# Longer weight part buffers, and a 32-byte offset for the parts of some stationary weight blocks

## The chip, the cores and the metric

The kernel runs on one core of a Trainium2 chip. The metric is the device time of one execution in microseconds (us), as the median of several runs; one more execution was recorded by the hardware profiler.

## The reference, cut to what matters

Two decoder layers on 256 tokens of width 2048. Layer 0 is a Mamba-2 mixer, layer 1 a sparse attention mixer; each ends in a residual and a layer norm. Nearly all the work is matrix products in float32 with large weights that are used once:

```
proj = x @ w_in                 # 2048 x 10304 (layer 0)
...                             # conv, scan by chunks, gate, group norm
h0 = yg @ w_out                 # 4096 x 2048
x1 = layer_norm(alpha * x + h0)
proj = x1 @ w_in                # 2048 x (512 + 336 + 4096): q and kv latents, gates
q, q_lat, o = small products per head with w_uq, w_uk, w_uv (32 heads)
out = layer_norm(alpha * x1 + (o * silu(gate)) @ w_out)   # 4096 x 2048
```

## The kernel before, in words

**Units.** All large weights come as a stream of 404 blocks ("units") of 128 partitions by 1024 float32 values (672 for the kv latent). The class `Stream` loads each into a `raw` buffer (pool `wraw`, four buffers), and `convert` makes two parts of it in a format that TensorE multiplies at a higher rate than float32: `hi`, a rounded copy made by ScalarE (L98), and `lo`, the rest, made by VectorE (L106). `hi` and `lo` lie in pools `whi` and `wlo` of four buffers each, so unit i uses the fifth, sixth ... buffer again in turn (i modulo 4). Some units around the two layer ends get their parts from pools of their own (`st.homes`: pools `wmore`, six buffers, and `wlast`, four): the last two blocks of the first output product, the first four of the q latent, the first two of the kv latent, and the last four of the second output product.

**How a unit is used on TensorE.** A matmul has a stationary operand (128 columns, loaded ahead by a weight load) and a moving operand that streams past it. There are two kinds of unit:

- *Stationary units* (`stream_w`: the input projection of layer 0, tile `acc`, and the gates of layer 1, tile `g`; also `idx_pe`, `pair_b` and the first half of `pair_a`): slices of 128 columns of `hi` and `lo` are the weights, the activations move. In `stream_w` a unit has eight matmuls of `hi` against 512 moving columns (L285) and eight of `lo` against 256 (L282). Two units make one output: the first runs `hi` and then `lo`, the second `lo` and then `hi`. The next pair so begins with `hi` where the last one ended with `hi`.
- *Moving units* (`out_proj`, L512 to L514, and `stream_tok`, L640 to L642): the activations are the weights, and 512 columns of `hi` or `lo` move (336 for the kv latent; 256 in the tail). The change calls these units "wide".

In `pair_a` the first 512 columns of the unit are stationary (key, L822 to L824) and the others move in slices of 256 (value, L831 to L833).

**What sets the order.** The order is written out: the program runs unit after unit, and smaller steps (convolution, norms, heads) are stepped in between. TensorE executes its list in that order.

**Where the operands lie.** Byte addresses within a partition, as the built program has them, taken modulo 64:

| operand | start modulo 64 before | after |
|---|---|---|
| `hi`, `lo` in `whi`, `wlo` (four buffers each) | 0 | 0, or 32 for the units that the change moves |
| `hi`, `lo` in `wmore`, `wlast` | 32 | 0 |
| activations of `stream_w` and of `out_proj` (`xT`, `x1T`, `yg`, `og`) | 0 | 0 |
| latents (`cqT`, `ckvT`), head operands (`hk`, `hq`, `hv`, `prT`) | 32 | 32 |

The slices that a matmul takes of them begin whole multiples of 64 bytes further on. Before, all buffers of `raw`, `hi` and `lo` and the activations `xT` start at the same place modulo 4096 as well; after, the four buffers of a pool start 64 bytes further on from one to the next, modulo 4096.

Of the kernel before, what the change touches and what calls it, by code (L numbers as in the profile page):

```python
# [10 lines left out]
F32R = mybir.dt.float32r  # L11
# [5 lines left out]
P = 128  # L17
# [34 lines left out]
EARLY = 8  # L52
# [5 lines left out]
class Unit:  # L58


    def __init__(self, src, width, pe):
        self.src, self.width, self.pe = src, width, pe


class Stream:
# [7 lines left out]
        self.limit = 1 << 30  # L73
        self.homes = {}

    def add(self, src, width, pe):
        self.units.append(Unit(src, width, pe))
        return len(self.units) - 1

    def side(self, i, gen):  # L80
        self.starts.setdefault(i, []).append(gen)
# [8 lines left out]
    def convert(self, i, eng, later=False):  # L90

        if i < len(self.units):
            w = self.units[i].width
            r = self.raws.pop(i)
            ph, pl = (self.homes[i],) * 2 if i in self.homes else (self.whi, self.wlo)
            h = ph.tile([P, 1024], F32R, tag="hi", name=f"hi{i}")
            l = pl.tile([P, 1024], F32R, tag="lo", name=f"lo{i}")
            self.nc.scalar.activation(h[:, :w], r[:, :w], AF.Copy)  # L98
            self.parts[i] = (h, l)
            self.halfway[i] = (l[:, :w], r[:, :w], h[:, :w].bitcast(F32))  # L100
        if not later:
            self.finish(i, eng)
# [34 lines left out]
def trunk_kernel(ctx: ExitStack, tc: tile.TileContext, x, xt, w1, wdt, dtp, prm, wo1,  # L137
# [14 lines left out]
    st = Stream(nc, wraw, whi, wlo)  # L152
    v = nc.vector

    def acc_tile(name):
        return p_acc.tile([P, 512], F32, tag="acc", name=name)
# [112 lines left out]
    def stream_w(half, cell, name):  # L269


        def pe(h, l):
            if half == 0:
                cell["ps"] = acc_tile(name)
            ps, xs = cell["ps"], cell["x"][0]
            first, second = (0, 1) if half == 0 else (1, 0)
            for lo in (first, second):
                for k in range(8):
                    kt, w = half * 8 + k, slice(k * P, (k + 1) * P)
                    last = half == 1 and lo == second and k == 7  # L280
                    if lo:
                        nc.tensor.matmul(ps[:, 0:T], l[:, w], xs[:, kt, 0:T], start=False,  # L282
                                         stop=last, skip_group_check=True)
                    else:
                        nc.tensor.matmul(ps, h[:, w], xs[:, kt, :], start=(kt == 0), stop=last,  # L285
                                         skip_group_check=True)
        return pe
# [194 lines left out]
    for g in range(NG):  # L482
        for kind, n in (("B", 1), ("C", 1), ("x", 4), ("z", 4)):
            for ci in range(n):
                cell = {"x": xcell}
                for half in range(2):
                    k = len(st.units)
                    i = st.add(w1[k], 1024, stream_w(half, cell, f"acc{k}"))
# [7 lines left out]
    def out_proj(arr, act, name, evac, lead, tail, hold):  # L496

        cells = [{} for _ in range(4)]  # L500

        def mm(n, kb, h, l, half, part=None, cols=(0, 512), first=0):

            c0, c1 = cols
            ps = cells[n]["ps"][half][:, c0:c1] if part is None else part
            for k in range(2):
                kk = kb * 2 + k
                a = act[kk // 16][:, kk % 16, :]
                ah = a[:, half * P:(half + 1) * P]
                al = a[:, T + half * P:T + (half + 1) * P]  # L510
                hs, ls = h[:, k * 512 + c0:k * 512 + c1], l[:, k * 512 + c0:k * 512 + c1]
                nc.tensor.matmul(ps, ah, hs, start=(kk == 2 * first), stop=False)  # L512
                nc.tensor.matmul(ps, ah, ls, start=False, stop=False)  # L513
                nc.tensor.matmul(ps, al, hs, start=False, stop=(kk == 31))  # L514

        held = []

        def unit(n, kb):
            def pe(h, l):
                if kb == 0:  # L520
                    mk = (acc_tile, y_tile)[n % 2]
                    cells[n]["ps"] = [mk(f"{name}{n}_{j}") for j in range(2)]
                mm(n, kb, h, l, 0)
                if n == 3 and kb >= 16 - hold:
                    held.append((n, kb, h, l))
                    if kb == 15:
                        tail(cells[n], held, mm)
                else:
                    mm(n, kb, h, l, 1)
            i = st.add(arr[n * 16 + kb], 1024, pe)  # L530
            if kb == 15 and n < 3:
                for half in range(2):
                    st.side(i, (evac, n, half, cells[n]))

        for n in (0, 1):
            for kb in range(lead):
                unit(n, kb)
        for n in (0, 1):
            for kb in range(lead, 16):
                unit(n, kb)  # L540
        for n in (2, 3):
            for kb in range(16):
                unit(n, kb)
# [87 lines left out]
    def stream_tok(kb, width, cell, name, held=None):  # L631

        def mm(kb, h, l, half):
            ps = cell["ps"][half][:, 0:width]
            for k in range(2):
                kt = kb * 2 + k
                ah = X1[0][:, kt, half * P:(half + 1) * P]
                al = X1[0][:, kt, T + half * P:T + (half + 1) * P]
                hs, ls = h[:, k * width:(k + 1) * width], l[:, k * width:(k + 1) * width]
                nc.tensor.matmul(ps, ah, hs, start=(kt == 0), stop=False)  # L640
                nc.tensor.matmul(ps, ah, ls, start=False, stop=False)
                nc.tensor.matmul(ps, al, hs, start=False, stop=(kt == 15))  # L642

        def pe(h, l):
            if kb == 0:
                cell["ps"] = [acc_tile(f"{name}{j}") for j in range(2)]
            mm(kb, h, l, 0)
            if held is None:
                mm(kb, h, l, 1)
                return  # L650
            held.append((kb, h, l))
            L["early"](kb)
            if len(held) == EARLY:
                for a in held:
                    mm(*a, 1)
                st.limit = 1 << 30
                st.convert_to(n_o1 + EARLY + 4)
        return pe
# [78 lines left out]
    cells = {"kv": {}, "q": {}}  # L737
    held = []
    for kb in range(8):
        i = st.add(wcq[kb], 1024, stream_tok(kb, 512, cells["q"], "qp",  # L740
                                             held if kb < EARLY else None))
    st.side(i, (lat_norm, cells["q"], 512, PC_QG, 4, "q", "cqT"))
    for kb in range(8):
        i = st.add(wkv[kb], 672, stream_tok(kb, 336, cells["kv"], "kvp"))
    st.side(i, (lat_norm, cells["kv"], 256, PC_KVG, 2, "kv", "ckvT"))
    st.side(i, (kidx_steps, cells["kv"]))
    gates = iter(range(NH2))
# [4 lines left out]
    def idx_pe(q, cell):  # L752
        def pe(h, l):
            cell["ps"] = acc_tile(f"ix{q}")
            for k in range(2):
                ps = cell["ps"][:, k * T:(k + 1) * T]
                for kt in range(4):
                    o = (k * 4 + kt) * P
                    nc.tensor.matmul(ps, h[:, o:o + P], cqT[:, kt, 0:T], start=(kt == 0), stop=False)
                    nc.tensor.matmul(ps, h[:, o:o + P], cqT[:, kt, T:2 * T], start=False, stop=False)  # L760
                    nc.tensor.matmul(ps, l[:, o:o + P], cqT[:, kt, 0:T], start=False, stop=(kt == 3))
        return pe
# [41 lines left out]
    for q in range(4):  # L804
        cell = {}
        i = st.add(wix[q], 1024, idx_pe(q, cell))
# [30 lines left out]
    def pair_b(p):  # L837
        def pe(h, l):
            pq = s_tile(f"q{p}")
            for k in range(2):  # L840
                ps = pq[:, k * T:(k + 1) * T]
                for kt in range(4):
                    o = (k * 4 + kt) * P
                    nc.tensor.matmul(ps, h[:, o:o + P], cqT[:, kt, 0:T], start=(kt == 0), stop=False)  # L844
                    nc.tensor.matmul(ps, h[:, o:o + P], cqT[:, kt, T:2 * T], start=False, stop=False)  # L845
                    nc.tensor.matmul(ps, l[:, o:o + P], cqT[:, kt, 0:T], start=False, stop=(kt == 3))  # L846
            PR[p]["pq"] = pq
        return pe
# [88 lines left out]
    for p in range(NH2 // 2):  # L937
        src = wab[2 * p]
        i = st.add(wab[2 * p], 1024, pair_a(p))
        st.side(i, (evac_steps, p, ("k", "v")))  # L940
        i = st.add(wab[2 * p + 1], 1024, pair_b(p))
# [3 lines left out]
        n = (left * (p + 1)) // 16 - (left * p) // 16  # L945
# [337 lines left out]
```

## Time and profile before

| | |
|---|---|
| median of 3 runs | 1241.61 us (1241.29 to 1241.68) |
| the profiled execution | 1241.89 us, of which 1240.2 us from the first to the last instruction |
| TensorE busy | 1229.6 us |
| VectorE, ScalarE, GpSimd busy | 938.6, 701.2, 68.1 us |
| weights and inputs read | 231 MB, 190 GB/s over the span |

The span is the time between the first and the last recorded instruction; 1.7 us of the profiled execution lie around it. In the rows below PE is TensorE's matmul, PEld its weight load, DVE VectorE, ACT ScalarE, POOL GpSimd, SP the engine that issues the loads of weights. A matmul's recorded duration holds the time in which its results drain, which overlaps the next one; what a matmul costs in a stream is the distance from its start to the next start, called its step here.

### The profile page before, as it was taken

What the parts mean: (1) busy time and instruction counts of PE and PEld (TensorE: products, weight loads), DVE (VectorE), ACT (ScalarE), POOL (GpSimd) and SP (SyncE); (2) the same over time, 40 slices, a digit from 0 to 9 for tenths busy, and PEclk for the clock granted to TensorE, in tenths of its full rate; (3) what the DMA queues carried; (4) which work ended last, traced back from release to release, by engine and by line L of the source; (5) the groups of instructions that cost most, each with busy time, mean ns of one, the idle gap of its engine ahead of it and who ended that gap; (6) DMA issues with size and microseconds to landing.
All of it is one profiled execution on the core that took longest, in us unless ns stands there. A gap on an engine that the chain in (4) does not pass through costs nothing.

```text
span 1240.2 us, 19396 instructions
## 1 busy us (share of the span) xinstructions
PE 1229.6 (99%) x7142; PEld 1067.1 (86%) x7142; DVE 938.6 (76%) x1753; ACT 701.2 (57%) x1272; POOL 68.1 (5%) x104
## 2 busy tenths in 40 slices
PE   8999999999999999999999999999999999999998
PEld 6888888888888888888888898999999999888886
DVE  6978788898889889856556768877777777667457
ACT  5566665666666666544335655476666666433341
POOL 1000001010110011110000000000000000000000
PEclk9999999999999999999999999999999999999999
DMA  7666666566757565677666564454444455875652
GB/s 277 208 195 186 194 183 211 168 207 181 220 151 221 173 216 170 198 214 243 197 192 204 179 217 148 160 184 154 156 152 154 155 169 164 329 221 187 203 189 99
DMA packets 65293, 236.53 MB, mean 191 GB/s; under 512 B 7912, under 2 KB 7920, under 8 KB 64816
## 3 DMA queue, kind: packets, MB, share of 16 engines
q1 hardware_dynamic: 60192, 215.12, 54.4%
q0 software_dynamic: 5008, 20.19, 5.0%
q8 instruction: 56, 0.92, 0.3%
q14 instruction: 37, 0.30, 0.1%
HBM read 231.00 MB, written 4.28 MB: 190 GB/s over the span
## 4 chain that ended last, share of the span: by engine, by line
PE 96%; DVE 2%; DMA 1%; issue 0%; ACT 0%; DVEq 0%; SPq 0%
PE acc L285 23%; PE acc L282 12%; PE g L285 10%; PE o L512 9%; PE o L514 9%; PE o L513 9%; PE g L282 5%; PE y L410 2%; PE q L846 1%; PE q L844 1%; PE q L845 1%; DVE lo L106 1%; PE pt L907 1%; PE p_dt L593 1%; PE pxs L390 1%; PE v L833 1%
## 5 line engine op out<-in xcount | busy, mean ns | idle before, releaser
L106 DVE TENSOR_TENSOR lo<-raw,hi 128x1024 fp32r<-128x1024 f32 (+1 forms) x404 | 489.6, 1214 | 245.8 <-ACT hi L98 245.3
L98 ACT ACTIVATE hi<-raw 128x1024 fp32r<-128x1024 f32 (+1 forms) x404 | 421.3, 1050 | 209.0 <-PE o L514 161.7
L285 PE MATMUL acc<-xT,hi 128*128 128x512 f32 x1280 | 314.2, 394 | 0.0
L285 PEld LDWEIGHTS acc<-xT,hi 128*128 128x128 f32 x1280 | 233.5, 188 | 45.6 <-ACT E L365 0.9
L282 PEld LDWEIGHTS acc<-xT,lo 128*128 128x128 f32 x1280 | 164.5, 191 | 6.3
L282 PE MATMUL acc<-xT,lo 128*128 128x256 f32 x1280 | 167.7, 283 | 0.0
L285 PE MATMUL g<-x1T,hi 128*128 128x512 f32 x512 | 127.7, 395 | 0.0
L285 PEld LDWEIGHTS g<-x1T,hi 128*128 128x128 f32 x512 | 92.6, 188 | 18.1 <-issue 0.2
L512 PE MATMUL o<-hi,yg 128*128 128x512 f32 x256 | 100.4, 392 | 0.0
L514 PE MATMUL o<-hi,yg 128*128 128x512 f32 x256 | 99.7, 389 | 0.0
L513 PE MATMUL o<-lo,yg 128*128 128x512 f32 x256 | 99.7, 389 | 0.0
L512 PE MATMUL o<-hi,og 128*128 128x512 f32 (+1 forms) x256 | 99.6, 389 | 0.0
L514 PE MATMUL o<-hi,og 128*128 128x512 f32 (+1 forms) x256 | 98.9, 386 | 0.0
L513 PE MATMUL o<-lo,og 128*128 128x512 f32 (+1 forms) x256 | 98.8, 386 | 0.0
L312 DVE SCALAR_TENSOR_TENSOR ca<-cr,convh,ca 128x255 f32<-128x255 f32 x144 | 69.2, 481 | 3.4
L282 PE MATMUL g<-x1T,lo 128*128 128x256 f32 x512 | 71.2, 284 | 0.0
L315 ACT ACTIVATE cr<-ca 128x256 f32<-128x256 f32 x48 | 20.1, 418 | 88.5 <-DVE ca L312 88.5
L282 PEld LDWEIGHTS g<-x1T,lo 128*128 128x128 f32 x512 | 67.2, 190 | 2.8
L514 PEld LDWEIGHTS o<-hi,yg 128*128 128x128 f32 x256 | 48.1, 188 | 10.2
L512 PEld LDWEIGHTS o<-hi,yg 128*128 128x128 f32 x256 | 48.1, 188 | 10.1 <-issue 0.2
L513 PEld LDWEIGHTS o<-lo,yg 128*128 128x128 f32 x256 | 48.1, 188 | 9.9
L514 PEld LDWEIGHTS o<-hi,og 128*128 128x128 f32 x256 | 48.1, 188 | 9.9
(265 smaller groups left out, 1781.0 us busy)
## 6 DMA issues: line engine op xcount, KB each, us to landing
raw<-in_w_dram SPq DMA_DIRECT2D x160, 512.0 KB, 4.1
raw<-in_wo_dram SPq DMA_DIRECT2D x128, 512.0 KB, 3.8
raw<-in_wg_dram SPq DMA_DIRECT2D x64, 512.0 KB, 3.3
raw<-in_wab_dram SPq DMA_DIRECT2D x32, 512.0 KB, 3.3
abc<-acs_d POOLq DMA_DIRECT2D x32, 256.0 KB, 4.2
raw<-in_wcq_dram SPq DMA_DIRECT2D x8, 512.0 KB, 4.6
raw<-in_wkv_dram SPq DMA_DIRECT2D x8, 336.0 KB, 3.2
rx<-in_x_dram POOLq DMA_DIRECT2D x2, 1024.0 KB, 11.6
```

Of the source, the lines that this page charges most:

```text
L98: self.nc.scalar.activation(h[:, :w], r[:, :w], AF.Copy)
L106: eng.tensor_sub(*self.halfway.pop(i))
L282: nc.tensor.matmul(ps[:, 0:T], l[:, w], xs[:, kt, 0:T], start=False, stop=last, skip_group_check=True)
L285: nc.tensor.matmul(ps, h[:, w], xs[:, kt, :], start=(kt == 0), stop=last, skip_group_check=True)
L312: v.scalar_tensor_tensor(acc[:, d:], rw[:, :T - d], w(k), acc[:, d:], op0=ALU.mult, op1=ALU.add)
L315: nc.scalar.activation(rw, acc, AF.Tanh)
L390: nc.tensor.transpose(pm[:, o:o + P], G[g][("x", 2 * half + c)][:, s * P:(s + 1) * P], ident)
L410: nc.tensor.matmul(py[ks, c * T + s * P:(c + 1) * T], xsT[:, s, c, ks], ms[c][k][:, ws], start=(c == 0 and s == 0), stop=(s == 1), skip_gr ...
L512: nc.tensor.matmul(ps, ah, hs, start=(kk == 2 * first), stop=False)
L513: nc.tensor.matmul(ps, ah, ls, start=False, stop=False)
L514: nc.tensor.matmul(ps, al, hs, start=False, stop=(kk == 31))
L593: nc.tensor.matmul(p_dt[0:NH1, 0:T], w_dt[:, kt, :], xr[:, kt, :], start=(kt == 0), stop=(kt == KT - 1))
```

## The change

Every `hi` and `lo` buffer gets 1040 columns instead of 1024 (64 bytes more). A unit's parts start at an offset in it: 0 for moving units; for stationary unit i, `hi` starts 32 bytes (8 values) further in where i // 4 is odd, and `lo` where i // 8 is odd; for units with homes both start 32 bytes further in. Nothing else is changed. No engine's list of instructions changes: the rows of the five engines are the same, in the same order, with the same shapes; only addresses differ. All other tiles behind these pools move by whole multiples of 64 bytes.

```
-    def __init__(self, src, width, pe):
-        self.src, self.width, self.pe = src, width, pe
+    def __init__(self, src, width, pe, at):
+        self.src, self.width, self.pe, self.at = src, width, pe, at
...
-    def add(self, src, width, pe):
-        self.units.append(Unit(src, width, pe))
-        return len(self.units) - 1
+    def add(self, src, width, pe, wide=False):
+
+        i = len(self.units)
+        at = (0, 0) if wide else (8 * (i // 4 % 2), 8 * (i // 8 % 2))
+        self.units.append(Unit(src, width, pe, at))
+        return i
...
-            h = ph.tile([P, 1024], F32R, tag="hi", name=f"hi{i}")
-            l = pl.tile([P, 1024], F32R, tag="lo", name=f"lo{i}")
+            a, b = (8, 8) if i in self.homes else self.units[i].at
+            h = ph.tile([P, 1040], F32R, tag="hi", name=f"hi{i}")[:, a:a + 1024]
+            l = pl.tile([P, 1040], F32R, tag="lo", name=f"lo{i}")[:, b:b + 1024]
...
-            i = st.add(arr[n * 16 + kb], 1024, pe)
+            i = st.add(arr[n * 16 + kb], 1024, pe, wide=True)
...
-                                             held if kb < EARLY else None))
+                                             held if kb < EARLY else None), wide=True)
...
-        i = st.add(wkv[kb], 672, stream_tok(kb, 336, cells["kv"], "kvp"))
+        i = st.add(wkv[kb], 672, stream_tok(kb, 336, cells["kv"], "kvp"), wide=True)
```

Counted in the built programs, the matmuls by the start of their operands modulo 64 (moving, stationary):

| matmuls | before | after |
|---|---|---|
| L285, 512 columns | 1792 at (0, 0) | 912 at (0, 0), 880 at (0, 32) |
| L282, 256 columns | 1792 at (0, 0) | 912 at (0, 0), 880 at (0, 32) |
| L512 to L514 and L640 to L642, 512 columns | 1512 at (0, 0), 96 at (32, 0) | 1608 at (0, 0) |
| L512 to L514 in the tail, 256 columns | 48 at (32, 0) | 48 at (0, 0) |
| L640 to L642, 336 columns | 72 at (0, 0), 24 at (32, 0) | 96 at (0, 0) |
| L759 to L761, L822 to L824, L844 to L846, 256 columns | 672 at (32, 0) | 336 at (32, 0), 336 at (32, 32) |
| L831 to L833, 256 columns | 192 at (0, 32) | 96 at (0, 32), 96 at (32, 32) |

## Rows read from the trace of the kernel before

**Rows 1.** The first part of the page: busy time of each engine, its share of the span, and instructions; and of the second part the granted TensorE clock in 40 slices, in tenths.

```profile
PE 1229.6 (99%) x7142; PEld 1067.1 (86%) x7142; DVE 938.6 (76%) x1753; ACT 701.2 (57%) x1272; POOL 68.1 (5%) x104
PEclk9999999999999999999999999999999999999999
```

**Rows 2.** The chain of work that ended last, first its shares by engine and then the first of its shares by line.

```profile
PE 96%; DVE 2%; DMA 1%; issue 0%; ACT 0%; DVEq 0%; SPq 0%
PE acc L285 23%; PE acc L282 12%; PE g L285 10%; PE o L512 9%; PE o L514 9%; PE o L513 9%; PE g L282 5%; PE y L410 2%; PE q L846 1%; PE q L844 1%; PE q L845 1%; DVE lo L106 1%; PE pt L907 1%; PE p_dt L593 1%; PE pxs L390 1%; PE v L833 1%
```

**Rows 3.** All waits of TensorE's matmuls: who waited for whom, us in total, times, longest.

```profile
PE p_dt L593 <- DMA scr<-in_xt_dram: 5.3, 1, 5.3
PE x1t L985 <- ACT rx L977: 0.3, 1, 0.3
PE cb L339 <- DVE C L321: 0.2, 1, 0.2
```

**Rows 4.** Groups of instructions by line and shape: count, busy us, mean ns of one, idle time before them.

```profile
L106 DVE TENSOR_TENSOR lo<-raw,hi 128x1024 fp32r<-128x1024 f32 x396 | 483.0, 1222 | 244.0 <-ACT hi L98 243.5
L98 ACT ACTIVATE hi<-raw 128x1024 fp32r<-128x1024 f32 x396 | 415.5, 1056 | 203.5 <-PE o L514 161.7 <-PE acc L285 10.3 <-DMA raw<-in_wo_dram 9.2
```

**Rows 5.** The chain in order of time, a stretch of the input projection of layer 0 (both operands at 0 modulo 64): start us, us, what, count. A piece lasts until the next piece starts.

```profile
118.02 1.91 PE acc L282 x16
119.94 3.65 PE acc L285 x16
123.59 1.91 PE acc L282 x16
```

**Rows 6.** The same view in the stage of the heads, gates of layer 1.

```profile
839.07 3.69 PE g L285 x16
```

**Rows 7.** Matmuls in order of time in the first output product, moving `hi` and `lo` at 0 modulo 64: start us, recorded us, line. There are nine starts from the first row to the last, the last one not counted.

```profile
560.16 0.39 PE L513 MATMUL o<-lo,yg 128*128 128x512 f32 x1
560.38 0.39 PE L514 MATMUL o<-hi,yg 128*128 128x512 f32 x1
560.61 0.39 PE L512 MATMUL o<-hi,yg 128*128 128x512 f32 x1
...
562.20 0.39 PE L513 MATMUL o<-lo,yg 128*128 128x512 f32 x1
```

**Rows 8.** The same view at the q latent: the first four units have moving parts at 32 modulo 64 (24 starts from the first row to the row at 685.77, where the first unit from `whi` and `wlo` begins), then 0 modulo 64 (nine starts to the row at 687.85, three more to the last).

```profile
680.17 0.40 PE L640 MATMUL qp<-hi,x1T 128*128 128x512 f32 x1
680.41 0.39 PE L641 MATMUL qp<-lo,x1T 128*128 128x512 f32 x1
680.64 0.40 PE L642 MATMUL qp<-hi,x1T 128*128 128x512 f32 x1
...
685.77 0.40 PE L640 MATMUL qp<-hi,x1T 128*128 128x512 f32 x1
...
687.85 0.39 PE L640 MATMUL qp<-hi,x1T 128*128 128x512 f32 x1
...
688.53 0.39 PE L640 MATMUL qp<-hi,x1T 128*128 128x512 f32 x1
```

**Rows 9.** The same view at the end of the second output product: moving parts at 32 modulo 64, first 512 columns (21 starts from the first row to the second), then 256 columns (40 starts from the third row to the fourth).

```profile
1213.32 0.40 PE L512 MATMUL o<-hi,og 128*128 128x512 f32 x1
...
1218.22 0.40 PE L512 MATMUL o<-hi,og 128*128 128x512 f32 x1
...
1224.40 0.28 PE L512 MATMUL o<-hi,og 128*128 128x256 f32 x1
...
1229.07 0.28 PE L513 MATMUL part<-lo,og 128*128 128x256 f32 x1
```

**Rows 10.** The same view at a head pair's queries: moving `cqT` at 32 modulo 64, stationary parts at 0, 256 columns; 21 starts from the first row to the last.

```profile
831.13 0.28 PE L846 MATMUL q<-cqT,lo 128*128 128x256 f32 x1
...
833.58 0.28 PE L846 MATMUL q<-cqT,lo 128*128 128x256 f32 x1
```

**Rows 11.** The same view at a head pair's values: moving parts at 0 modulo 64, stationary `ckvT` at 32, 256 columns; twelve starts from the first row to the last.

```profile
784.79 0.28 PE L831 MATMUL v<-hi,ckvT 128*128 128x256 f32 x1
784.90 0.28 PE L832 MATMUL v<-lo,ckvT 128*128 128x256 f32 x1
785.02 0.28 PE L833 MATMUL v<-hi,ckvT 128*128 128x256 f32 x1
...
786.21 0.28 PE L844 MATMUL q<-cqT,hi 128*128 128x256 f32 x1
```

**Rows 12.** The same view at a head's output and at another head's logits: both operands at 32 modulo 64, 256 columns.

```profile
823.23 0.28 PE L917 MATMUL o<-prT,hv 128*128 128x256 f32 x1
823.34 0.28 PE L918 MATMUL o<-prT,hv 128*128 128x256 f32 x1
823.45 0.28 PE L919 MATMUL o<-prT,hv 128*128 128x256 f32 x1
823.57 0.38 PE L920 MATMUL o<-prT,hv 128*128 128x128 f32 x2
...
830.66 0.28 PE L882 MATMUL lg<-hk,hq 128*128 128x256 f32 x1
830.77 0.28 PE L883 MATMUL lg<-hk,hq 128*128 128x256 f32 x1
830.90 0.28 PE L844 MATMUL q<-cqT,hi 128*128 128x256 f32 x1
```

**Rows 13.** The same view at a unit of the kv latent, 336 columns: three matmuls with slices at the start of the parts, three with slices 1344 bytes further in (21 times 64), and both again for the other 128 tokens.

```profile
717.90 0.31 PE L640 MATMUL kvp<-hi,x1T 128*128 128x336 f32 x1
...
718.36 0.31 PE L640 MATMUL kvp<-hi,x1T 128*128 128x336 f32 x1
...
718.82 0.31 PE L640 MATMUL kvp<-hi,x1T 128*128 128x336 f32 x1
...
719.27 0.31 PE L640 MATMUL kvp<-hi,x1T 128*128 128x336 f32 x1
...
719.73 0.39 PE L285 MATMUL g<-x1T,hi 128*128 128x512 f32 x1
```

## The prediction

> **What bounds the kernel now.** I read the busy times first: TensorE is busy 1229.6 us of 1240.2, at full granted clock (its upper level, 2.4 GHz) from end to end [rows 1]. The chain that ended last is TensorE's for 96% [rows 2], and its matmuls wait for other engines and for transfers 5.8 us in all, nearly all of it once at the start [rows 3]. So the time is the sum of the steps of 6,872 matmuls, and only a change in a step, or a wait that comes new, can move it. The third view is therefore the order of time on TensorE, read as distances between starts. ScalarE's and VectorE's conversions are 1056 and 1222 ns per block and sit behind waits of 203.5 and 243.5 us, that is, they idle [rows 4].
>
> The steps of equal matmuls are not equal, and what differs is where their operands start. With 512 moving columns: both operands at 0 modulo 64 gives (562.20 - 560.16) / 9 = 226.7 ns in a settled stream [rows 7]; moving operand at 32 gives (685.77 - 680.17) / 24 = 233.3 ns at the q latent [rows 8] and (1218.22 - 1213.32) / 21 = 233.3 in the tail [rows 9]. With 256 columns it is the other way: both at 0 gives 1.91 us / 16 = 119.4 ns [rows 5]; moving operand at 32 gives 2.45 / 21 = 116.7 in the queries [rows 10] and 4.67 / 40 = 116.8 in the tail [rows 9]. Then there is settling: where the q latent goes from 32 to 0 modulo 64, the next nine steps are still (687.85 - 685.77) / 9 = 231.1 ns, and only those behind them 0.68 / 3 = 226.7 [rows 8]. The long matmuls of the input projection are at 3.65 / 16 = 228.1 ns [rows 5], those of the gates at 3.69 / 16 = 230.6 [rows 6]: half of them come right behind short ones and are settling.
>
> **The change part by part.** It moves no instruction, so it adds no wait and takes none away; it moves addresses.
>
> *Long matmuls of stationary units (L285).* 880 of 1792 get a stationary operand at 32 under a moving one at 0. No row shows that with 512 columns. The nearest is the same difference the other way round, 233.3 ns [rows 8, 9]; the other end is that they settle at 226.7 as aligned ones do. The mean now is (1280 x 228.1 + 512 x 230.6) / 1792 = 228.8. So the term is between 880 x (226.7 - 228.8) = -1.8 us and 880 x (233.3 - 228.8) = +4.0 us. I take +4.0: a 32-byte difference between the two operands is what the slow rows have, and they go on unsettled for 24 steps.
>
> *Settling when the offset goes back.* `hi` is moved for four units, then not for four: 1792 / 64 = 28 returns. The first unit after one now follows settled `hi` matmuls, and then follows unsettled ones: nine steps at 231.1 instead of 226.7, 40 ns each time, +1.1 us at most, 0 if nothing unsettles. I take +0.7, since part of these units already restart behind other work.
>
> *Short matmuls of stationary units (L282).* 880 of 1792 get the offset. The row with the stationary operand off and the moving one on is the values': 1.42 / 12 = 118.3 ns [rows 11], a short run of mixed operands; the long runs with a 32-byte difference give 116.7. From 119.4 that is 880 x -1.1 = -1.0 us or 880 x -2.7 = -2.4 us. I take the middle, -1.7. The lower bound comes from the heads' outputs, where both operands are at 32: (823.57 - 823.23) / 3 = 113.3 ns [rows 12], which would be -5.4 us; three matmuls behind another stream are a weak witness.
>
> *Units with homes.* 96 moving matmuls of 512 columns go from 32 to 0: from 233.3 to 226.7, -0.6 us, less what they take to settle, so -0.5. The 48 short ones in the tail go the other way, 116.8 to 119.4, +0.1. For 336 columns I take nothing: 24 matmuls at 6.6 ns, the largest difference above, would be 0.2 us.
>
> *Queries, keys and index (336 matmuls) and values (96).* They come to have both operands at 32. If it is the difference that counts, queries, keys and index lose their gain: 336 x 2.7 = +0.9 us. The rows with both at 32 say 113.3 and, at the logits, (830.90 - 830.66) / 2 = 120 ns [rows 12], so from -1.1 to +1.1; I take half, +0.5. Values move by 96 x 1.1 = 0.1.
>
> *Steps of 64 bytes between buffers.* The 1,512 aligned long matmuls of moving units, and the unmoved half of the stationary ones, change their difference by multiples of 64 bytes. No row shows this with 512 columns. With 336, three matmuls take 0.46, 0.46, 0.45 and 0.46 us, whether their slices lie an odd number of 64 bytes further in or not [rows 13]; I take 0. If it unsettled them at every second buffer, 756 x (231.1 - 226.7) = +3.3 us.
>
> *Conversions.* ScalarE writes and VectorE reads and writes at the new places. A change of 1% in 1222 ns over 404 blocks is 4.9 us of VectorE time, under the 243.5 us that it waits for ScalarE, and TensorE waits for neither outside the start [rows 3, 4]. Without that cover, a late `lo` would hold L282 first; nothing here comes near. I take 0.
>
> Sum: +4.0 + 0.7 - 1.7 - 0.5 + 0.1 + 0.5 = +3.1 us, with a lean against it: of the unknown terms, the first one decides, and its upper end is the one I took. Weighting that term at +3.6 (the moving rows may overstate it, since the values' row lies between aligned and shifted) gives +2.7. On the profiled execution, 1241.9 becomes 1244.6; it stands 0.3 us over the median of the runs, so on the median 1241.6 + 2.7 = 1244.3.
>
> A rule of the Trainium skill is weighed here against the rows. The page "TensorE: Matmul & The Clock Gate", section "Step-by-step: what each phase is for", says that TensorE reads moving and stationary operands through two independent ports, so that loading the next weights takes nothing from the running matmul. By it the stationary offset would cost and bring nothing, all terms but that of the homes would be 0, and the sum -0.5. The values' 118.3 ns against 119.4 speaks against it, weakly; no run of before tries it with 512 columns. It is the first rival below.
>
> **The rivals.**
> - *The offset of the stationary operand does nothing.* Then only the moving operand's place counts, the homes give -0.5 and the time is 1241.1. For it: in every long run with a 32-byte difference it is the moving operand that is off [rows 8 to 10]. Against it: it would have to slow 512 columns and speed up 256, and rows 11, with a moving operand at 0, are not at 119.4 either.
> - *Faster: the stationary offset brings the gain of the short ones and none of the loss of the long ones.* Place: L282 at 116.7, -2.4; L285 settles at once behind the short ones, -1.8; homes -0.5: -4.7, so 1236.9. With L285 left as it is, 1238.7. It decides from a step of L285 under 230 ns in the moved units: then the short ones' gain outweighs. For it: no row shows (0, 32) with 512 columns, and rows 12 have 113.3. Against it: the q latent's steady 233.3.
> - *Slower by more: the 64-byte steps unsettle the moving units too.* +3.3 on top, 1247.6. For it: every settled long row has its operands at the same place in all larger multiples of 64 bytes too (up to 512), so none has tried it; against it: rows 13.
>
> **How the numbers follow.** The trade of long against short: 0.55, with a range of its own from +0.5 to +4.5, 1242.1 to 1246.1. No effect: 0.15. Faster: 0.23. The 64-byte price: 0.07. A measurement of this kernel tells about 0.2%, 2.5 us, from no change. The trade lies across that bound: slower in 0.31 of its 0.55, same in 0.24. With the rivals: faster 0.23, same 0.39, slower 0.38. The range leaves out a tenth at each side: from the faster rival's 1237.0 to 1247.0, short of the 64-byte rival.
>
> **What would show it right or wrong.** In the chain in order of time, units with `hi` moved should have L285 at 16 x 233.3 = 3.73 us for a pair's joined `hi` matmuls instead of 3.65, and those with `lo` moved should have L282 at 1.87 to 1.89 instead of 1.91, with the pattern repeating every 16 units. The q latent's first 24 steps should take 5.45 us instead of 5.60. The first output product should stay at 226.7. It is wrong if L285's moved units are at 226.7 or under 230, if L282 does not move, if steps of moving units change with the buffer, or if TensorE shows a new wait.

## The result, and the profile after

The changed kernel takes 1250.88 us (median of 6 runs, 1250.28 to 1251.46), beside 1241.67 us for the kernel before on the same chip (1241.29 to 1241.91). The ratio is 1.0073 [1.0062, 1.0083]: 9.2 us slower. The forecast was 1244.3 us with a range to 1247.0; the time lies outside it, beyond the slowest rival's 1247.6 as well. The profiled execution took 1250.86 us, of which 1249.2 us are span.

The first part of the page after (busy time, share, instructions), then the shares by engine and by line of the chain that ended last, then all waits of TensorE. Lines past L120 stand four further on than before: L285 is now L289, L282 is L286, L512 to L514 are L516 to L518.

```profile
PE 1238.9 (99%) x7142; PEld 1065.9 (85%) x7142; DVE 938.4 (75%) x1753; ACT 701.6 (56%) x1272; POOL 67.8 (5%) x104
```

```profile
PE 99%; DVE 0%; DMA 0%; DVEq 0%; issue 0%; SPq 0%
PE acc L289 24%; PE acc L286 12%; PE g L289 10%; PE o L517 9%; PE o L516 9%; PE o L518 9%; PE g L286 5%; PE y L414 2%; PE q L848 1%; PE q L850 1%; PE q L849 1%; PE pt L911 1%; PE p_dt L597 1%; PE pxs L394 1%; PE v L836 1%; PE v L835 1%
```

```profile
PE p_dt L597 <- DMA scr<-in_xt_dram: 5.3, 1, 5.3
```

Against [rows 1 to 3], TensorE is busy 9.3 us longer, the chain is still TensorE's, and no wait is new. All of the loss lies in the steps of its matmuls. The sum over the steps of all 6,872 matmuls, taken from their starts in the two traces, grew from 1228.98 to 1237.92 us, +8.9 of the span's +9.0. It divides so (the homes' -0.5 and +0.1 shared by count between latents and output products):

| matmuls | predicted, us | measured, us |
|---|---|---|
| L285, 880 moved by 32 bytes | +4.0 | +3.7 |
| L285, 912 not moved | +0.7 | +1.7 |
| L282, 880 moved | -1.7 | -1.0 |
| L282, 912 not moved | 0 | -2.3 |
| L512 to L514, both output products | -0.15 | **+5.7** |
| latents | -0.25 | +0.1 |
| queries, keys, index | +0.5 | +0.8 |
| values | +0.1 | +0.1 |

L512 to L514, which have no 32-byte offset anywhere, carry the miss. The other groups come to +3.1 where +3.35 was predicted, but by luck in part: the unmoved L285 and L282 missed in opposite directions. The chain in order of time, a stretch of the input projection (start us, us, what, count), beside [rows 5]:

```profile
151.31 3.73 PE acc L289 x16
155.04 1.91 PE acc L286 x16
156.94 3.70 PE acc L289 x16
160.64 1.86 PE acc L286 x16
...
166.86 1.87 PE acc L286 x16
168.73 3.72 PE acc L289 x16
```

L285 takes 3.70 to 3.73 us where it took 3.65, L282 1.86 to 1.91 where it took 1.91. The predicted 3.73 and 1.87 to 1.89 are there, but also outside the moved units: in the L286 rows at 160.64 and 166.86 `lo` is not moved and still takes 1.86 and 1.87, and of the 3.72 at 168.73 half of the `hi` matmuls are not moved. Now the first output product, whose matmuls were at 226.7 ns [rows 7]; the first matmul of five units that follow each other, 12 steps each (start us, recorded us, line):

```profile
563.59 0.39 PE L516 MATMUL o<-hi,yg 128*128 128x512 f32 x1
...
566.38 0.39 PE L516 MATMUL o<-hi,yg 128*128 128x512 f32 x1
...
569.17 0.39 PE L516 MATMUL o<-hi,yg 128*128 128x512 f32 x1
...
571.93 0.39 PE L516 MATMUL o<-hi,yg 128*128 128x512 f32 x1
...
574.67 0.39 PE L516 MATMUL o<-hi,yg 128*128 128x512 f32 x1
```

Four units, four steps: 2.79 / 12 = 232.5 ns twice, 2.76 / 12 = 230.0, 2.74 / 12 = 228.3. The pattern goes with the buffer, i modulo 4, and 64 bytes is what the buffers differ by. That "steps of moving units change with the buffer" was one of the signs of being wrong that the prediction named. The recorded duration is 0.39 us throughout; only the distance between starts shows the loss.

In what follows, "distance" is the start of the moving operand less that of the stationary one, in bytes modulo 256. The four units above have distances 192, 128, 64 and 0. The starts are those of the built programs. Mean steps by group are worked out from all starts of a trace, gaps over a quarter above the group's median left out; sums of a group keep them.

### The profile page after: what moved, and what is told of

It reads as the page before. It is cut to its first block, busy times and chain, and to the rows that moved or that the text cites. A ratio compares the mean times of both kernels' runs of the same rounds, so it can differ in the third digit from the quotient of the medians.

```text
span 1249.2 us, 19396 instructions
## 1 busy us (share of the span) xinstructions
PE 1238.9 (99%) x7142; PEld 1065.9 (85%) x7142; DVE 938.4 (75%) x1753; ACT 701.6 (56%) x1272; POOL 67.8 (5%) x104
## 4 chain that ended last, share of the span: by engine, by line
PE 99%; DVE 0%; DMA 0%; DVEq 0%; issue 0%; SPq 0%
PE acc L289 24%; PE acc L286 12%; PE g L289 10%; PE o L517 9%; PE o L516 9%; PE o L518 9%; PE g L286 5%; PE y L414 2%; PE q L848 1%; PE q L850 1%; PE q L849 1%; PE pt L911 1%; PE p_dt L597 1%; PE pxs L394 1%; PE v L836 1%; PE v L835 1%
## 5 line engine op out<-in xcount | busy, mean ns | idle before, releaser
L289 PE MATMUL acc<-xT,hi 128*128 128x512 f32 x1280 | 318.6, 397 | 0.0
L289 PEld LDWEIGHTS acc<-xT,hi 128*128 128x128 f32 x1280 | 233.1, 188 | 49.1 <-ACT E L369 0.9
L286 PEld LDWEIGHTS acc<-xT,lo 128*128 128x128 f32 x1280 | 162.1, 188 | 7.1
L286 PE MATMUL acc<-xT,lo 128*128 128x256 f32 x1280 | 165.0, 280 | 0.0
L289 PE MATMUL g<-x1T,hi 128*128 128x512 f32 x512 | 128.7, 397 | 0.0
L289 PEld LDWEIGHTS g<-x1T,hi 128*128 128x128 f32 x512 | 92.5, 188 | 18.6 <-issue 0.2
L516 PE MATMUL o<-hi,yg 128*128 128x512 f32 x256 | 101.1, 395 | 0.0
L518 PE MATMUL o<-hi,yg 128*128 128x512 f32 x256 | 100.6, 393 | 0.0
L516 PE MATMUL o<-hi,og 128*128 128x512 f32 (+1 forms) x256 | 100.2, 391 | 0.0
L518 PE MATMUL o<-hi,og 128*128 128x512 f32 (+1 forms) x256 | 99.7, 390 | 0.0
L286 PE MATMUL g<-x1T,lo 128*128 128x256 f32 x512 | 70.6, 282 | 0.0
L286 PEld LDWEIGHTS g<-x1T,lo 128*128 128x128 f32 x512 | 66.6, 188 | 3.1
L516 PEld LDWEIGHTS o<-hi,yg 128*128 128x128 f32 x256 | 48.1, 188 | 11.2 <-ACT hi L102 0.3
L518 PEld LDWEIGHTS o<-hi,yg 128*128 128x128 f32 x256 | 48.1, 188 | 11.0
L518 PEld LDWEIGHTS o<-hi,og 128*128 128x128 f32 x256 | 48.1, 188 | 10.6
```

## The experiments

**The buffers' length alone.** The change without its 32-byte offsets:

```
-        at = (0, 0) if wide else (8 * (i // 4 % 2), 8 * (i // 8 % 2))
+        at = (0, 0)
-            a, b = (8, 8) if i in self.homes else self.units[i].at
+            a, b = self.units[i].at
```

> Only the 64 bytes more per buffer; every part starts at 0 in its buffer, parts in home pools stay at 32 modulo 64. Theory A (a step depends on the distance between the starts of moving and stationary operand, modulo 128 or more): the moving units stay as slow as in the changed kernel (L512 to L514 near 231 ns, +5.7 us over before), the short stationary ones (L282) get faster in half of the units, near 117 ns (-4.7 us), the long ones (L285) go to 231 (+3.6 us): 1246 us. Theory B (any distance that is a whole multiple of 64 settles, the loss comes from the distance changing from one unit to the next): moving units near 231 too, L282 and L285 as before or slightly slower: 1247 to 1249 us. Theory C (only the 32-byte offsets cost, as the prediction had it): 1241.6 us.

Measured: 1247.38 us (1247.3 to 1248.42) beside 1242.03, ratio 1.0046 [1.0029, 1.0063], +5.35 us. L512 to L514 gained 5.8 us, as in the changed kernel, L285 +2.7, L282 -4.7, queries, keys and index +1.0. The chain in the input projection, then two units of the first output product:

```profile
153.71 1.87 PE acc L286 x16
155.57 3.69 PE acc L289 x16
159.26 1.86 PE acc L286 x16
```

```profile
561.87 0.39 PE L516 MATMUL o<-hi,yg 128*128 128x512 f32 x1
...
564.67 0.39 PE L516 MATMUL o<-hi,yg 128*128 128x512 f32 x1
...
567.44 0.39 PE L516 MATMUL o<-hi,yg 128*128 128x512 f32 x1
```

Units take 2.80 / 12 = 233.3 and 2.77 / 12 = 230.8 ns with nothing moved by 32 bytes. By distance, L512 to L514 have mean steps of 229.2 (0), 229.4 (64), 232.4 (128) and 233.3 (192); L282 has 119.0, 114.4, 118.2 and 114.9. So the 64 bytes that the forecast priced at nothing cost more than the rest of the change.

**Is it the drift from buffer to buffer, or the distance itself?** The kernel before, with unused bytes ahead of `whi`, so that all of `hi` and `lo` lie a constant distance further in: 64 bytes (16 columns, as here), 32 (8) or 256 (64). The buffers stay 4096 bytes long.

```
+    gap = ctx.enter_context(tc.tile_pool(name="gap", bufs=1))
+    gap.tile([P, 16], F32, tag="gap", name="gap")
```

> The kernel before, with 64 unused bytes ahead of the hi buffers: all parts 64 bytes further in, the same for every unit. Theory A: L282 falls from 119.4 to about 114 ns as in the changed kernel's units with that distance (-9.7 us), L285 and L512 to L514 are between 226.7 and 233.3: 1232 to 1247 us. Theory B: nothing changes, since the distance is constant and a multiple of 64: 1241.6 us, L512 to L514 settled at 226.7, L282 at 119.4.

Measured with 64 bytes: 1244.0 us (1243.19 to 1244.94), ratio 1.0017 [1.0006, 1.0027]. The chain, and units of the output product six starts apart:

```profile
153.36 1.82 PE acc L284 x16
155.18 3.73 PE acc L287 x16
158.91 1.82 PE acc L284 x16
```

```profile
561.78 0.39 PE L514 MATMUL o<-hi,yg 128*128 128x512 f32 x1
...
563.15 0.39 PE L514 MATMUL o<-hi,yg 128*128 128x512 f32 x1
...
564.52 0.39 PE L514 MATMUL o<-hi,yg 128*128 128x512 f32 x1
```

The distance does not change from buffer to buffer here, and still all three groups moved: L285 (distance 192) from 229.0 to 233.0 ns, its single steps in turns of 231 and 236; L282 (192) from 119.5 to 114, 1.82 us for 16; the output products (64) to 1.37 / 6 = 228.3 here, 229.1 in the mean. The total is small because +6.6 us in L285 and +2.8 in the output products meet -8.6 in L282. A constant multiple of 64 is not neutral.

> The kernel before, with 32 unused bytes ahead of the hi buffers: every part 32 bytes further in, the same for every unit. Theories A and B (the distance counts): L282 near 117 ns (-4.8 us), L285 near 233.3 (+8 us), L512 to L514 at 233.3 (+10 us), homes aligned (-0.6 us): 1254 us. Theory D (only the moving operand's own start counts): L282 and L285 unchanged, L512 to L514 at 233.3: 1251 us.

Measured with 32 bytes: 1255.4 us (1255.24 and 1255.55), ratio 1.0108 [1.0087, 1.0128].

```profile
151.21 3.73 PE acc L287 x16
154.94 1.90 PE acc L284 x16
```

L285 and L282 are at distance 224 and take 232.9 and 118.6 ns, the output products, at 32, 233.2. L282 so gave 1.5 us, where 4.8 were expected. In L285 and L282 the moving operand, `xT`, lies where it did; only the stationary one moved, and the step of the running matmuls changed. So the moving operand's own place is not all that counts. Nor is it the place of either by itself: in this run and the one before, the queries, keys, index and values have both operands 32 or 64 bytes further in, their distance is as before, and so are their steps, 117.0 (116.8 before) and 118.3 ns (118.3).

> The kernel before, with 256 unused bytes ahead of the hi buffers: all parts 256 bytes further in. The theory now (A2: a step depends on the distance between moving and stationary start modulo 256): nothing changes, L285 at 228 to 231, L282 at 119.4, L512 to L514 at 226.7, 1242 us. Rival (A3: modulo 512 or more, or the place within a larger block): another set of steps, L512 to L514 off 226.7, anything from 1232 to 1255 us.

Measured with 256 bytes: 1242.47 us (1240.94 to 1242.87) beside 1241.95, ratio 1.0004 [0.9993, 1.0014], and every group's mean step as before to 0.2 ns.

```profile
150.10 3.65 PE acc L287 x16
153.75 1.91 PE acc L284 x16
```

These are the 3.65 and 1.91 of [rows 5]. The dependence repeats after 256 bytes, and not after 128: L285 takes 233.0 ns at a constant distance of 192 (all parts 64 bytes in) and 229.5 at one of 64 (a run below).

**`lo` moved and `hi` not.** The unused bytes stand between `whi` and `wlo`: 64 (as here), then 192 (48 columns). The pools behind `wlo` move with it, so the latents come to another distance from `hi`, and the homes from the activations.

```
     whi = ctx.enter_context(tc.tile_pool(name="whi", bufs=SPLIT))
+    gap = ctx.enter_context(tc.tile_pool(name="gap", bufs=1))
+    gap.tile([P, 16], F32, tag="gap", name="gap")
     wlo = ctx.enter_context(tc.tile_pool(name="wlo", bufs=SPLIT))
```

> The kernel before, with 64 unused bytes between the hi and the lo buffers: only the lo parts 64 bytes further in. Theory A: L282 about 114 ns (-9.7 us), L285 as before, L513 with another distance than its neighbours L512 and L514, so these three do not settle, near 231 (+6.5 us): 1238 us. Theory B: L282 at 119.4 as before; L512 to L514 either settle or not, 1241.6 to 1248 us.

Measured with 64 bytes: 1247.98 us (1247.28 to 1249.03), ratio 1.005 [1.0034, 1.0066].

```profile
153.26 1.89 PE acc L284 x16
155.15 3.65 PE acc L287 x16
158.80 1.89 PE acc L284 x16
```

L285 uses `hi`, and stays at 3.65. But L282, at distance 192 as in the run with all parts 64 bytes in, is at 117.4 ns and not at 114. The output products, whose matmuls alternate between distance 0 (`hi`) and 64 (`lo`), are at 232.0, slower than with all of them at 64 (229.1). The queries, keys and index, now at 96 with `hi` and still at 32 with `lo`, rose from 116.8 to 119.6 (+1.8 us). Neither theory holds as it stood: L282 moved, against B, and by less than A said. So a step depends also on the distances of the matmuls around it.

> The kernel before, with 192 unused bytes between hi and lo buffers: moving start minus lo start is 64 modulo 256 in L282. A2, with the steps of the units that had this distance in e1_stride (113.3 ns): -10.9 us from L282, +6.5 to +7.5 us from L512 to L514, whose lo no longer fits their hi: 1238 us. Rival (what settles depends on what ran before: behind settled long matmuls the short ones stay at 117.4 as in e4_lo64): 1246 to 1248 us.

Measured with 192 bytes: 1244.2 us (1243.09 to 1244.88), ratio 1.0018 [1.0008, 1.0028].

```profile
153.99 1.89 PE acc L284 x16
155.88 3.69 PE acc L287 x16
```

The time lies between the two forecasts. L282 is at distance 64 and takes 117.8 ns; L285, whose operands all lie as before, takes 230.4 instead of 229.0 in the input projection (and 228.9 instead of 230.2 in the gates), behind short matmuls that now run at another distance. The distance within L282 alone does not set its step: behind `hi` at distance 0 it stays near 117.5, at 192 in the run before and at 64 here. With the longer buffers, where `hi` and `lo` of a unit share their distance, it was at 114.4 and 114.9, although the distance there changes from unit to unit. The output products rose to 229.1 only, +2.8 us where 6.5 to 7.5 were expected; why 0 and 192 in turns costs less than 0 and 64 in turns is not shown.

**The 32-byte offsets without the drift.** Buffers of 1088 columns are 17 x 256 bytes long, so the distance does not go with the buffer. They need room; both this run and its control have three `raw` buffers instead of four.

```
-RAW = 4
+RAW = 3
```

> Control for the next: the kernel before with three raw buffers instead of four, which frees 4096 bytes; all distances modulo 256 as before. TensorE waits for no load in the kernel before, so 1241.5 to 1243 us; if the loads come late, more, with waits of L98 for loads that it did not have.

Measured, the control: 1244.91 us (1243.91 to 1245.84), ratio 1.0026 [1.0016, 1.0037]. It was expected free of cost and is not. The mean steps are those of before; waits of TensorE are new, 8.8 us in all instead of 5.8, and each output product takes 1 us more. The longest:

```profile
PE p_dt L593 <- DMA scr<-in_xt_dram: 5.6, 2, 5.4
PE cb L339 <- DVE C L321: 1.1, 1, 1.1
PE x1t L985 <- DVE rx L979: 1.0, 1, 1.0
PE o L513 <- DVE lo L106: 0.8, 1, 0.8
```

So the run with the offsets is read against this one:

```
+            a, b = (8, 8) if i in self.homes else self.units[i].at
+            h = ph.tile([P, 1088], F32R, tag="hi", name=f"hi{i}")[:, a:a + 1024]
+            l = pl.tile([P, 1088], F32R, tag="lo", name=f"lo{i}")[:, b:b + 1024]
```

> The change's offsets of 32 bytes without the drift of 64 bytes from buffer to buffer: buffers of 1088 columns (256 bytes more, so that all four start alike modulo 256), three raw buffers to make room. The prediction's own sum, which this run isolates: L285 in moved units at 233, L282 in moved units at 117 to 118, moving units settled at 226.7: +2.7 us over the control, 1244 to 1246 us. Rival (the offsets are the cause of all of it, the drift of none): +9 us, 1251 us. Rival (the drift is the cause of all): the control's time.

Measured: 1247.94 us (1247.11 to 1248.44), ratio to before 1.0049 [1.0034, 1.0064]; 3.0 us over the control.

```profile
152.00 3.74 PE acc L289 x16
155.74 1.89 PE acc L286 x16
157.63 3.70 PE acc L289 x16
161.33 1.91 PE acc L286 x16
```

```profile
562.16 0.39 PE L516 MATMUL o<-hi,yg 128*128 128x512 f32 x1
...
564.88 0.39 PE L516 MATMUL o<-hi,yg 128*128 128x512 f32 x1
...
567.60 0.39 PE L516 MATMUL o<-hi,yg 128*128 128x512 f32 x1
```

The output product is back at 2.72 / 12 = 226.7 ns. What is left is the change that the forecast had priced: L285 moved +3.05 us, not moved +0.5, L282 moved -0.9, not moved -0.3, queries, keys and index +0.5, values +0.1, latents -0.1, together +2.9.

**A version from this.** The long matmuls of the output products want distance 0; in the input projection and the gates the short ones gain more at 64 than the long ones lose. So the weights stay as before, and the activations `xT` and `x1T` move 64 bytes in, while `yg` and `og` in the same buffers do not:

```
-    xT = big.tile([P, KT, 2 * T], F32R, tag="A", name="xT")
+    def wide_tile(name, tag, at):
+        t = big.tile([P, KT * 2 * T + 64], F32R, tag=tag, name=name)
+        return t[:, at:at + KT * 2 * T].rearrange("p (k t) -> p k t", k=KT)
+    xT = wide_tile("xT", "A", 16)
...
+        X1.append(wide_tile("x1T", "B", 16))
```

> The kernel before, with the activations that move past stationary units (xT, x1T) 64 bytes further in and the weight parts where they were: distance 64 modulo 256 in L285 and L282, 0 still in L512 to L514. From the units with this distance in the changed kernel and in e1_stride: L282 at 113.3 to 114.5 ns instead of 119.4 (-9 to -11 us), L285 at a steady 229 without settling instead of 228.8 on average (0), moving units settled at 226.7 (0): 1231 to 1233 us. Rival (what ran before decides, as in e4_lo64): L282 at 117.5, -3.5 us, 1238.5 us.

Measured: **1238.58 us** (1237.69 to 1239.48) beside 1242.48, ratio 0.9969 [0.9957, 0.9981]: 3.9 us faster than the kernel before.

```profile
153.61 1.88 PE acc L286 x16
155.49 3.68 PE acc L289 x16
159.17 1.81 PE acc L286 x16
```

```profile
562.21 0.39 PE L516 MATMUL o<-hi,yg 128*128 128x512 f32 x1
...
564.93 0.39 PE L516 MATMUL o<-hi,yg 128*128 128x512 f32 x1
```

L282 settles in one of two ways at the same distance: 1.81 / 16 = 113.1 ns and 1.88 / 16 = 117.5, both within the input projection. The larger gain expected, 9 to 11 us, would have needed 113 throughout; L282 gave 5.8 us. The total is the rival's 1238.5, though L282's mean, 115.3 in the input projection, is not the rival's 117.5. What goes with the one or the other can be read from the starts: L285 runs here in turns of about 226, 229 and 232 ns, and of the 79 runs of L282 straight behind L285, 40 of the 41 where L285's last step, up to the first start of L282, was 231 or 232 settle at 113, and all 38 where it was 225 to 230 settle near 118. That is an association within one trace; no run tests it, and with `lo` 192 bytes further in all 79 stay near 118. The output products keep 226.7.

On top of it, 32 unused bytes ahead of the homes, the latents and the head operands:

```
+    d1.tile([P, 8], F32, tag="gap", name="gap")
```

> As the run before it, and 32 unused bytes ahead of the home pools, the latents and the head operands: the queries', keys' and index's matmuls come to distance 64, the values' to 192, the homes' moving parts to 64 or 0 instead of 32. By the steps seen so far: queries, keys, index 480 + 192 matmuls from 116.8 to 113.5 (-2.2 us), values from 118.3 to 113.5 (-0.9 us), homes from 233.3 to 229 or 226.7 (-0.5 us): 3 to 4 us less than e9_act64. If what ran before decides: less than 1 us.

Measured: 1238.82 us (1238.39 to 1239.15), ratio 0.9972 [0.9961, 0.9983]; no gain beyond the last, as its rival had it. The values fell from 118.3 to 116.1 ns and the latents from 233.3 to 230.2, the queries rose from 116.9 to 117.6: each less than 1 us in sum.

The steps of the runs without drift beside each other, mean ns in the input projection and the first output product, distance in brackets:

| run | L285, 512 columns | L282, 256 columns | L512 to L514, 512 columns |
|---|---|---|---|
| before; all +256 | 229.0 (0) | 119.5 (0) | 227.1 (0) |
| all +64 | 233.0 (192) | 114.2 (192) | 229.1 (64) |
| all +32 | 232.9 (224) | 118.6 (224) | 233.2 (32) |
| `lo` +64 | 229.0 (0) | 117.4 (192) | 232.0 (0, 64 in turns) |
| `lo` +192 | 230.4 (0) | 117.8 (64) | 229.0 (0, 192 in turns) |
| `xT`, `x1T` +64 | 229.5 (64) | 115.3 (64) | 227.1 (0) |

## Why the prediction was wrong

*What bounds the kernel.* Right, and so is the settling: behind L282, L285's first steps in the input projection of the kernel before are 233, 236, 228, 232 and 231 ns, and then 227 (medians over 50 runs of 16). The sum of steps makes the time, before and after, and the one wait of TensorE in the changed kernel is the first of [rows 3]; a conversion was late nowhere in it.

*Steps of 64 bytes between buffers.* This is the step that failed: "three matmuls take 0.46, 0.46, 0.45 and 0.46 us [...]; I take 0". Measured alone, the longer buffers cost +5.35 us. The rows used are of 336 columns, three matmuls each, and of another length: in all runs the 336-column steps have means between 152 and 157 ns at every distance, so rows of that length show next to nothing of the effect. For 512 columns the text itself said that no settled row had tried it, and then took the row that existed over the gap. The trace of the kernel before also held a row that spoke against it. In [rows 12] both operands start at 32 modulo 64 in the head's output and in the logits alike, and the steps are 113.3 and 120 ns; over all 32 heads the means are 114 to 115 and 117.5 to 119. In the built program their distances are 192 and 0. Two placements that are equal modulo 64 so differed by 3 to 6 ns, and the text took the one for a weak witness and the two together for bounds of another term. The bound was mis-sized as well: +3.3 put half of 1,512 matmuls at 231.1, and left out the short ones. In fact three of four distances are slower, 229.4 to 233.3, and the fourth, 0, no longer holds 226.7 but has 229.2, with each unit of 12 matmuls behind one at another distance. The 1,560 matmuls lost 5.7 us. L285's unmoved units took 1.7 us more in the changed kernel and L282's gave back 2.3; without drift these are +0.5 and -0.3, so the rest goes with the drift.

*The 32-byte offsets.* Right in every direction, and nearly in the sum: +3.0 us measured without drift, +2.7 to +3.1 forecast. That the sum fits so well is partly luck, as L285's term was 0.9 us too high and L282's gain 0.8 too large; the sum also left out its own +0.1 for the values. L285 moved +3.05 (+4.0: 3.5 ns each where 4.5 were taken), the settling at returns +0.5 (+0.7), L282 -0.9 (-1.7), queries, keys and index +0.5 (+0.5), values +0.1 (+0.1). Of the homes' gain the latents showed -0.1 where -0.25 was their part. In the changed kernel the q latent's first 24 steps took 5.55 us and not the 5.45 predicted: at 0 modulo 64 their distances were 64, 0, 192 and 128. In the last run above, where they are 0 modulo 256, they took 5.45.

*What is not accounted for.* 5.35 and 3.0 make 8.4 of the 9.2 us. The two are not quite additive (distances of 96 and 160, which only the changed kernel has, take 233.4 and 234.6 in L285); L285's moved units alone lost 0.6 us more than without drift. The remainder is within the intervals of the two.

*The rivals.* That the stationary offset does nothing is refuted: with 32 bytes on the stationary side alone, L285 and L282 go to 232.9 and 118.6. The rule of the Trainium skill named there, "TensorE: Matmul & The Clock Gate", section "Step-by-step: what each phase is for", by which the ports for moving and stationary operands are independent and a weight load takes no read bandwidth from the running matmul, would have left both steps as they were; these do not agree with it, and the measurement decides. The faster rival fell with L285's 3.74 us. The 64-byte rival, at 0.07, had the right place: the output products lost 5.7 us where it said 3.3. It had half of the mechanism, as the distance itself costs as well as its change: at a constant 64 they take 229.1.

## What to carry to other kernels

Where TensorE is the bound and its matmuls follow each other, with operands in this format and a weight load for each, as here, compare the start addresses of moving and stationary operands modulo 256 bytes, and keep buffers a multiple of 256 bytes long, so that the difference does not go round with the buffers. A row that is equal in the variable you think counts and differs in its step, as in [rows 12], says that the variable is another. Read the distance between starts, as the recorded duration of a matmul hides the effect. Where a forecast rests on rows of another shape because none of the right one exists, let the bound, not the row, set the range.

## What the runs showed of the hardware

- With both operands in this format and a weight load for every matmul, the step depends on the distance of the two operands' starts, and repeats after 256 bytes: a shift of 256 changed no group by over 0.2 ns. Both operands moved by the same 32 or 64 bytes left the steps of the queries, keys, index and values as they were, to 0.2 ns.
- The order is not that of alignment, and not the same for both lengths. 512 columns: 0 is best (226.7 ns when settled), then 64 (229), then 128, 192 and any odd multiple of 32 (mostly 232 to 235). 256 columns: 0 is among the slowest (119.5), 64 and 192 can reach 113, 128 and the odd multiples of 32 lie at about 117 to 120. 336 columns: 152 to 157 at every distance.
- The step depends on the matmuls around it as well: at distance 64, 256 columns settle at 113 in some runs of 16 and at 118 in others. Which of the two goes with the last step of the long matmuls ahead (113 behind 231 or 232 ns, 118 behind 225 to 230, in 78 of 79 runs of one trace); what causes it was not found, and no run shows why the period is 256 bytes.
